# All heads' values as one operand (high halves, a one, 63 low halves), the 64th low half summed on DVE, and more gates beside both attentions

## The chip, the cores and the metric

The kernel runs on one core of a Trainium2 chip. The metric is device time in microseconds of one execution. TensorE (PE) multiplies, PEld is its weight load, VectorE (DVE), ScalarE (ACT) and GpSimd (POOL) do the rest, SyncE (SP) issues nearly all DMAs. Matmul results lie in PSUM, in eight banks of 128 partitions by 512 numbers; everything else is in SBUF.

## The reference

Two layers of an encoder over 512 tokens and 1024 channels, all in float32. What matters here, shortened:

```python
def block_attention(q, k, v):                     # softmax over 512 keys
    sc = einsum(q, k) * dk ** -0.5
    return einsum(softmax(sc), v)
for l in range(2):
    h = rms_norm(x, attn_norm_g[l])
    c_q, c_kv, k_rope, gq, gk, gv, pool_in, gate_logits = split_columns(h @ w_in[l], IN_SIZES)
    o_mla = mla_branch(...)      # 8 heads, keys of 64 + 32, values of 64, made from low-rank latents
    o_gqa = gqa_branch(...)      # 8 query heads of 64, 2 key/value heads
    o_pool = pool_branch(...)    # centred means over 2, 4, 8, 16 tokens
    gates = sigmoid(gate_logits)                  # three gates of 1024 channels
    merged = (gates[0] * (o_mla @ w_branch_mla[l]) + gates[1] * (o_gqa @ w_branch_gqa[l])
              + gates[2] * (o_pool @ w_branch_pool[l]))
    x = x + merged @ w_out[l]
    u = depthwise_conv(rms_norm(x, ffn_norm_g[l]) @ ffn_w_up[l])
    x = x + (silu(u_gate) * u_val) @ ffn_w_down[l]
```

## The kernel before

**Numbers in two halves.** Every operand of a matmul is split into a rounded high half (an `F32R` copy, mostly by ACT) and a low half (the number minus its high half, by DVE or POOL). A product is three matmuls, high x high, high x low and low x high: the helper `mm3`. A weight arrives by DMA in pieces of up to 512 columns, two to a load (`w_dma`, on SP's queue), three loads ahead; `w_split` makes its halves `wh` and `wl`, three pieces ahead.

**One order, planned when the program is built.** Instructions are issued by a Python program that keeps a clock of its own (`Clock`). It has an estimated cost for each instruction and a heap of later steps: `chain(...)` puts the steps that follow a matmul (an ACT copy, then a DVE subtraction, and so on) at the times when the estimates let them start; `need(key)` moves the clock to when something is ready, `ps(tag)` to when a PSUM bank is free. So the order on every engine is fixed beforehand, and on the chip each engine runs its own list and waits on semaphores. The banks are named by tag: `acc` two, `ST` two, `AV` two, `S` one, `mi` one.

**A layer.** The input projection comes first: latents, pool channels, GQA queries, and GQA keys and values (`tok_major` for results by token, `feat_major` for results by channel). The norm's sum of squares `sq` is reduced by eight small matmuls (`norm_finish`), in layer 0 during the first pool group. Then come the three branches, and then output projection, up-projection with convolution, and down-projection.

**The attentions.** `attention(kind, fill, ...)` runs 8 heads. A head transposes its queries (`t_q`, and `t_k` in MLA), finds row maxima from high halves alone (`s_max`: four matmuls into `S`, each followed by a DVE reduction `nm`), folds them in (`m_row`), and for each of four key blocks computes scores into an `ST` bank (`probs`), takes the exponential there on ACT (`ex`), copies the high half `ph` (`hi`) and subtracts for the low half `pl` (`lo`), after which the bank is free. `av_hi` multiplies the values' high halves by `ph`, and in a second matmul of 64 columns their low halves by `ph`; `av_lo` multiplies the high halves by `pl`. All 12 matmuls of a head go to one `AV` bank:

```python
                mm(s["av"], vh, ph[:, :T], k == 0, False)
                mm(s["av"][0:64], vl, ph[:, :T], False, False)
                mm(s["av"], vh, pl[:, :T], False, k == 3)
```

`vh` holds 64 columns of value high halves and 64 columns of ones, so rows 64 to 127 of the bank are the softmax's denominators. `o_out` copies both parts out, and after each second head transposes the sums, takes reciprocals, multiplies, and splits the pair into an operand `oh`, `ol` of the branch's projection.

**Fillers beside them.** A `Filler` is a list of independent matmul groups that is stepped between the attention's own: a unit is one step, three matmuls of 512 columns in a gate or a branch. `gates(br, ...)` makes, for one branch, 8 gates `gate(m)` (8 units; DVE multiplies by the norm, ACT takes a tanh) and 8 branch projections `branch(m)` (4 units; a DVE product, an addition to `XM`, in the last branch a split and a DMA back of the old `XM`), interleaved by `_order(br)` with MLA's making of queries, key parts and values (`EXTRA`). Branch 2 (pool) runs beside the GQA attention; branch 1 (GQA) and 16 units of branch 0 (MLA) beside the MLA attention; the other 80 units of branch 0 after it. Positions of an attention's steps relative to its heads are in `PLAN`: one position is a quarter of a head. A step whose inputs are not ready by the clock lets the filler go ahead, by up to `SLACK` units.

Of the kernel before, what the change touches and what calls it, by code (L numbers as in the profile page):

```python
# [11 lines left out]
F32R = mybir.dt.float32r  # L12
# [18 lines left out]
RAW = 3  # L31
EXTRA = (("q", 2, (2, 5)), ("n", 2, (6, 7)), ("v", 1, (0, 3)))
PRO = 0.47
# [6 lines left out]
PLAN = {"gqa": (0.006, 0.786, 0.986, 0.65, 3.252, 2.411, 4.57, 32.003),  # L40
        "mla": (-2.351, 0.028, 1.098, 0.64, 3.303, 1.678, 1.82, 33.91)}
W_BIAS = 2.54
C_BIAS = 0.2
# [13 lines left out]
def _order(br):  # L57


    r, lag = [], 2 if br == 0 else 1  # L60
# [127 lines left out]
class Engine:  # L188
# [35 lines left out]

    def tensor_scalar(self, out, *a):
        self._count(out, *((0.0043, 0.2) if self.kind == "Pool" else (0.00055, 0.07)))
        return self.eng.tensor_scalar(out, *a)
# [19 lines left out]
def trunk(ctx: ExitStack, tc: tile.TileContext, x, w, prm, gb, cst, out):  # L247
# [57 lines left out]
    def w_split():  # L305
        j = st["split"]
        sl, off, wd = pieces[j]
        r = raws[sl][:, off:off + wd]
        hi = hlp.tile([P, T], F32R, tag="wh", name=f"wh{j}")
        lo = hlp.tile([P, T], F32R, tag="wl", name=f"wl{j}")  # L310
        ck.fin = ck.now
        A.activation(hi[:, :wd], r, AF.Copy)
        e = V if j < KC + 3 else pick(W_BIAS, ck.fin + ck.SEM)
        ck.free[e.kind] = max(ck.free.get(e.kind, 0.0), ck.fin + ck.SEM)
        e.tensor_tensor(lo[:, :wd], r, f(hi[:, :wd]), ALU.subtract)
        done("w", j)
        halves[j] = (hi, lo)
        st["split"] += 1
# [45 lines left out]
    ones = cp.tile([P, P], F32R, tag="ones", name="ones")  # L364
    mhalf = cp.tile([P, 1], F32, tag="mhalf", name="mhalf")


# [142 lines left out]
    def layer(l, sq, xsrc):  # L510
# [172 lines left out]
        gqb = [ps(t) for t in qtags]  # L683
        VG, KAB = [], []
        for b in range(4):
            v = slot("vg", F32R)
            vh = v[:, 0:256].rearrange("p (h f) -> p h f", f=P)
            vl = v[:, 256:384].rearrange("p (h f) -> p h f", f=64)
            VG.append((vh, vl))
        for j in range(2):  # L690
            KAB.append((slot("ka", F32R), slot("kb", F32R)))

        def set_ones():
            for vh, _ in VG:
                V.memset(f(vh[:, :, 64:P]), 1.0)
            for _, kb in KAB:
                V.memset(f(kb[64:68, :T]), 1.0)
# [85 lines left out]
        def kv_evac(b):  # L783
            vh, vl = VG[b]
            src = kvb[b][:, P:2 * P].rearrange("p (h f) -> p h f", f=64)
            A.activation(vh[:, :, 0:64], src, AF.Copy, scale=rtok(b))
            A.activation(krt[:, b, :], kvb[b][:, 2 * P:288], AF.Copy, scale=rtok(b))

            def lo():
                V.scalar_tensor_tensor(vl, src, rtok(b), f(vh[:, :, 0:64]), ALU.mult, ALU.subtract)  # L790
                free(ktags[b])
                done("vg", l, b)
            chain(lo, after=ck.fin - ck.now + 0.1)
# [92 lines left out]
        mla_make = {}  # L886
        VM = {}
        ss = small("ssm", [P, 2, 2, 4, 4])
        krr = small("krr", [P, 4, 32], bufs=1)
# [121 lines left out]
        def v_out(g, p, acc):  # L1011
            lo2 = slot("vml", F32R)
            vs = []
            for i in range(2):
                v = slot("vmh", F32R)
                vh = v[:, :T].rearrange("p (h f) -> p h f", f=P)
                lv = lo2[:, 256 * i:256 * i + 256].rearrange("p (h f) -> p h f", f=64)
                G.memset(f(vh[:, :, 64:P]), 1.0)
                VM[2 * p + i, g] = (vh, lv)
                vs.append((vh[:, :, 0:64], lv, acc[:, 256 * i:256 * i + 256].rearrange("p (h f) -> p h f", f=64)))  # L1020

            def hi():
                for vh, _, src in vs:
                    copy(vh, src)
# [12 lines left out]
        def attention(kind, fill, okey, odst):  # L1037
# [27 lines left out]
            def t_pair(h):  # L1065
# [7 lines left out]
                for i in range(2):  # L1073
# [5 lines left out]
                    def hi(qa=qa, own=own):  # L1079
                        copy(qa[own, :T], tp[own])  # L1080

# [62 lines left out]
            def probs(h, k):  # L1144
# [23 lines left out]
                def lo():  # L1168
                    V.tensor_tensor(pl[:, :T], sc, f(ph[:, :T]), ALU.subtract)
                    free("ST")  # L1170
                    done(*key("pl", h, k))

                chain(ex, hi, lo)

            def vals(h, k):
                if gqa:
                    need(("vg", l, k))
                    vh, vl = VG[k]
                    return vh[:, h // 4, :], vl[:, h // 4, :]
                need(("vm", l, k, h // 4))  # L1180
                vh, vl = VM[k, h // 4]
                return vh[:, h % 4, :], vl[:, h % 4, :]

            def av_hi(h, k):
                s = hs[h]
                need(key("ph", h, k))
                if k == 0:
                    s["av"] = ps("AV")
                vh, vl = vals(h, k)
                ph = s["p", k][0]  # L1190
                mm(s["av"], vh, ph[:, :T], k == 0, False)
                mm(s["av"][0:64], vl, ph[:, :T], False, False)

            def av_lo(h, k):
                s = hs[h]
                need(key("pl", h, k))
                vh, vl = vals(h, k)
                pl = s.pop(("p", k))[1]
                mm(s["av"], vh, pl[:, :T], False, k == 3)
                if k == 3:  # L1200
                    o_out(h)

            def o_out(h):
# [6 lines left out]
                def copies():  # L1210
                    A.activation(sums[js, :T], s["av"][64:128], AF.Copy)
                    A.activation(raw[js, :T], s["av"][0:64], AF.Copy)
                    free("AV")

                steps = [copies]
                if h % 2 == 1:
# [4 lines left out]
                    steps += [lambda: V.transpose(turned[:, :T], sums[:, :T]),  # L1221
                              lambda: V.reciprocal(inv, turned[:, :T].rearrange("p (b f) -> p b f", f=32)[:, :, 0]),
                              lambda: V.transpose(sums[:, :T].rearrange("p (b f) -> p b f", f=32),
                                                  bc(inv.unsqueeze(2), [P, 16, 32]))]
# [7 lines left out]
            for h in range(8):  # L1232
# [11 lines left out]
            def waits(fn, h, k=None):  # L1244
# [11 lines left out]
                if fn is av_hi:  # L1256
                    return [key("ph", h, k)], "AV" if k == 0 else None
                return [key("pl", h, k)] * (fn is av_lo), None

# [17 lines left out]

        fa = Filler(gates(2, "op", opool, "first"), units(2))
        fa.upto(PRE_A)
# [9 lines left out]
        attention("gqa", fa, "og", ogqa)  # L1289
        fc = Filler(gates(0, "om", omla, "last"), units(0))  # L1290

        def beside():

            yield from gates(1, "og", ogqa, "add")
            for _ in range(2 * KC):
                fc.step()
                yield
# [6 lines left out]
        fc.finish()  # L1304

# [126 lines left out]
    A.activation(warm, warm, AF.Exp)  # L1432
    V.memset(f(ones), 1.0)
    idle = ps("mi")
    for _ in range(9):
# [163 lines left out]
```

## Time and profile before

| | |
|---|---|
| median of three runs | 1649.69 us (1648.71 to 1650.75) |
| the profiled execution | 1649.25 us, span of its instructions 1647.3 us |
| PE busy | 1640.4 us, 7435 matmuls |
| DVE, ACT, POOL busy | 890.5, 761.8, 921.9 us |
| HBM read | 139.90 MB, 87 GB/s over the span with what is written |

The span is the time from the first to the last instruction on the core. In a row of groups the columns are engine, operation, tiles written and read (out<-in), shapes, count, then busy time and mean duration in ns, then the engine's idle time just before and what ended it. In a row of the timeline they are start, duration (us), engine, line, operation, tiles, count; what stands in brackets is idle time of the engine before it and who released it. In a table of windows each engine has its busy us and its count of instructions in that stretch.

### The profile page before, as it was taken

The numbers are of one execution on the slowest core, as the hardware profiler recorded it, in microseconds if no ns is written. First come the engines' busy times: TensorE is split into PE (matmuls) and PEld (weight loads), VectorE is DVE, ScalarE is ACT, GpSimd is POOL, SyncE is SP. The second block draws the span as 40 slices with busy tenths as digits, with TensorE's granted clock in tenths as the row PEclk, the third lists the DMA queues.
The fourth block names the chain that finished last, engine by engine and source line by source line (L and its number), as shares of the span: only waits on it lengthen the run. The fifth ranks groups of instructions, "written<-read, shape, count | busy, mean of one in ns | idle before, by whom it ended". The sixth has DMA issues, their size and how long they took to land.

```text
span 1647.3 us, 20363 instructions
## 1 busy us (share of the span) xinstructions
PE 1640.4 (100%) x7435; PEld 1336.7 (81%) x7435; DVE 890.5 (54%) x1404; ACT 761.8 (46%) x1357; POOL 921.9 (56%) x805
## 2 busy tenths in 40 slices
PE   9999999999999999999999999999999999999999
PEld 8887887778888888888888888877788888888888
DVE  6777756643366666621046677566332666666000
ACT  6457745543444444432244577455434444444221
POOL 3762763344666666654568538534446656656542
PEclk9999999999999999999999999999999999999999
DMA  5221121123322323333332211211243232332331
GB/s 201 82 84 46 60 65 48 52 71 118 119 90 90 103 90 91 102 102 122 102 103 89 82 39 62 74 39 52 85 133 95 85 103 90 91 101 90 126 111 45
DMA packets 44739, 145.40 MB, mean 88 GB/s; under 512 B 5088, under 2 KB 6624, under 8 KB 44640
## 3 DMA queue, kind: packets, MB, share of 16 engines
q1 hardware_dynamic: 44352, 143.97, 27.6%
q8 instruction: 59, 0.97, 0.2%
q14 instruction: 40, 0.33, 0.1%
q10 hardware_dynamic: 288, 0.14, 0.0%
HBM read 139.90 MB, written 4.19 MB: 87 GB/s over the span
## 4 chain that ended last, share of the span: by engine, by line
PE 98%; DVE 1%; ACT 1%; DMA 0%; SPq 0%; issue 0%
PE ps_acc L344 44%; PE ps_AV L344 24%; PE ps_ST L344 23%; PE ps_S L344 4%; PE ps_mi L344 2%; PE ps_mi L348 1%; DVE sq L215 0%; DMA XM<-x 0%; ACT wh L208 0%; ACT sqt L208 0%; DVE wl L215 0%; PE ps_acc L348 0%; SPq L301 0%; ACT HH L208 0%; SPq L1439 0%
## 5 line engine op out<-in xcount | busy, mean ns | idle before, releaser
L215 POOL TENSOR_TENSOR wl<-raw,wh 128x512 fp32r<-128x512 f32 (+2 forms) x508 | 662.9, 1315 | 589.0 <-ACT wh L208 457.7
L208 ACT ACTIVATE wh<-raw 128x512 fp32r<-128x512 f32 (+3 forms) x522 | 308.8, 607 | 125.6 <-PE ps_ST L344 41.1
L219 DVE SCALAR_TENSOR_TENSOR a<-u,prm,a 128x512 f32<-128x512 f32 x176 | 238.9, 1358 | 79.4 <-ACT a L208 73.2
L344 PE MATMUL ps_acc<-HH,wh 128*128 128x512 f32 x592 | 234.7, 396 | 1.4 <-DVE XM L219 1.4
L344 PE MATMUL ps_acc<-HL,wh 128*128 128x512 f32 x592 | 234.6, 396 | 0.0
L344 PE MATMUL ps_acc<-HH,wl 128*128 128x512 f32 x592 | 234.2, 396 | 0.0
L344 PEld LDWEIGHTS ps_acc<-HH,wh 128*128 128x128 f32 x592 | 111.5, 188 | 28.5 <-ACT mqs L208 1.7
L344 PEld LDWEIGHTS ps_acc<-HH,wl 128*128 128x128 f32 x592 | 111.3, 188 | 26.3
L344 PEld LDWEIGHTS ps_acc<-HL,wh 128*128 128x128 f32 x592 | 111.5, 188 | 25.5
L208 ACT ACTIVATE ps_ST<-ps_ST 128x512 f32<-128x512 f32 x128 | 74.6, 583 | 113.5 <-PE ps_ST L344 113.0
L344 PE MATMUL ps_AV<-HL,wh 128*128 128x512 f32 x288 | 114.2, 396 | 0.0
L344 PE MATMUL ps_AV<-HH,wl 128*128 128x512 f32 x288 | 114.2, 396 | 0.0
L344 PE MATMUL ps_AV<-HH,wh 128*128 128x512 f32 x288 | 113.6, 394 | 0.0
L223 DVE TENSOR_REDUCE nm<-ps_S 128x1 fp32r<-128x512 f32 x128 | 87.8, 686 | 42.4 <-PE ps_S L344 41.1
L215 DVE TENSOR_TENSOR pl<-ps_ST,ph 128x512 fp32r<-128x512 f32 x128 | 87.7, 685 | 38.4 <-ACT ph L208 37.4
L215 POOL TENSOR_TENSOR al<-a,ah 128x512 fp32r<-128x512 f32 x44 | 58.2, 1322 | 84.9 <-ACT ah L208 58.6
L344 PE MATMUL ps_ST<-HL,wh 128*128 128x512 f32 x240 | 95.3, 397 | 0.0
L344 PE MATMUL ps_ST<-HH,wl 128*128 128x512 f32 x240 | 95.0, 396 | 0.0
L344 PE MATMUL ps_ST<-HH,wh 128*128 128x512 f32 x240 | 94.6, 394 | 0.0
L208 ACT ACTIVATE a<-u,prm 128x512 f32<-128x512 f32 x88 | 71.8, 815 | 33.4 <-DVE u L215 33.4
L208 ACT ACTIVATE ah<-a 128x512 fp32r<-128x512 f32 x44 | 27.8, 631 | 116.0 <-DVE u L243 110.6
L208 ACT ACTIVATE a<-a 128x512 f32<-128x512 f32 x44 | 27.8, 632 | 113.0 <-DVE u L243 113.0
(361 smaller groups left out, 3543.8 us busy)
## 6 DMA issues: line engine op xcount, KB each, us to landing
raw<-w SPq DMA_DIRECT2D x228, 512.0 KB, 3.5
raw<-w SPq DMA_DIRECT2D x13, 384.0 KB, 3.1
XM<-x SPq DMA_DIRECT2D x16, 256.0 KB, 4.1
raw<-w SPq DMA_DIRECT2D x6, 448.0 KB, 3.4
xsp<-XM SPq DMA_DIRECT2D x8, 256.0 KB, 2.0
XM<-xsp SPq DMA_DIRECT2D x8, 256.0 KB, 3.4
out<-XM SPq DMA_DIRECT2D x7, 256.0 KB, 2.1
raw<-w SPq DMA_DIRECT2D x4, 432.0 KB, 3.1
```

Source lines behind the costliest of these rows:

```text
L208: return self.eng.activation(out, in_, func, **k)
L215: return self.eng.tensor_tensor(out, *a)
L219: return self.eng.scalar_tensor_tensor(out, *a)
L223: return self.eng.tensor_reduce(out, in_, *a, **k)
L344: PE.matmul(o, lhsT=lhsT, rhs=rhs, start=start, stop=stop)
L348: PE.transpose(o, src, ident)
```

## The change

Values: `vh` becomes one operand of 128 columns: 64 high halves, a single column of ones (64), and the low halves of value channels 1 to 63 (65 to 127). The low half of channel 0 goes to a small tile (`vg0`, `vm0`). `av_hi` and `av_lo` are one matmul each with this operand. Row 64 of the bank is then the denominator and rows 65 to 127 hold what is to be added to rows 1 to 63. The contribution of the 64th low half is summed over the key blocks by DVE from the scores in PSUM (`rest`, before the `ST` bank is freed) into a tile `t`, and one more matmul with `unit`, a matrix whose first column is ones, adds it to row 0 (`av_rest`). `o_out` sets the denominators' row in the copied lower part to zero, after the reciprocals, and adds it to the raw output (on GpSimd, for the last head on DVE); two small ACT copies spread the reciprocals.

Fillers: 24 units of branch 1 move beside the GQA attention, and 48 instead of 16 units of branch 0 stand beside the MLA attention (`SOONER`), with gates running further ahead of their projections (`LAG`), and the MLA values made with other gates (`EXTRA`).

Smaller edits: the first weight piece's high half is copied by DVE; for that piece (`use == 1` in `tok_major`: the first of eight channel blocks of layer 0's latents) the twelve matmuls run operand by operand, not bank by bank; layer 0's `norm_finish` comes two units later; the GQA queries' high half is always copied by ACT; `set_ones` and MLA's memsets write one column for 64.

```diff
-EXTRA = (("q", 2, (2, 5)), ("n", 2, (6, 7)), ("v", 1, (0, 3)))
+EXTRA = (("q", 2, (2, 5)), ("n", 2, (6, 7)), ("v", 1, (2, 5)))
+SOONER = {1: 3 * KC, 0: 6 * KC}
+LAG = {2: 1, 1: 4, 0: 6}
...
-        A.activation(hi[:, :wd], r, AF.Copy)
+        if j == 0:
+            V.tensor_copy(hi[:, :wd], r)
+        else:
+            A.activation(hi[:, :wd], r, AF.Copy)
...
+                if st["use"] == 1:
+                    for n, (x_, w_) in enumerate(((HH, wh), (HL, wh), (HH, wl))):
+                        for b in range(4):
+                            mm(banks[b][:, :wd], x_[:, kc, b * P:b * P + P], w_[:, :wd], n == 0, False)
+                    continue
...
-                if l == 0 and g == 0 and n == 3:
+                if l == 0 and g == 0 and n == 5:
...
-                for vh, lv, src in vs:
-                    V.tensor_tensor(lv, src, f(vh), ALU.subtract)
+                for vh, v0, src in vs:
+                    V.tensor_tensor(vh[:, :, 65:P], src[:, :, 1:64], f(vh[:, :, 1:64]), ALU.subtract)
+                for vh, v0, src in vs:
+                    V.tensor_tensor(v0, src[:, :, 0], f(vh[:, :, 0]), ALU.subtract)
...
-                        copy(qa[own, :T], tp[own])
+                        A.activation(qa[own, :T], tp[own], AF.Copy)
...
                 def lo():
                     V.tensor_tensor(pl[:, :T], sc, f(ph[:, :T]), ALU.subtract)
+                    done(*key("pl", h, k))
+                def rest():
+                    if k == 0:
+                        s["t"] = slot("vt", F32R)
+                        V.tensor_scalar(s["t"][:, :T], sc, vals(h, k)[1], None, ALU.mult, psum=True)
+                    else:
+                        t = s["t"][:, :T]
+                        V.scalar_tensor_tensor(t, sc, vals(h, k)[1], f(t), ALU.mult, ALU.add)
                     free("ST")
-                    done(*key("pl", h, k))
+                    if k == 3:
+                        done(*key("t", h))
-                chain(ex, hi, lo)
+                chain(ex, hi, lo, ([("vg", l, k) if gqa else ("vm", l, k, h // 4)], rest))
...
-                mm(s["av"], vh, ph[:, :T], k == 0, False)
-                mm(s["av"][0:64], vl, ph[:, :T], False, False)
+                mm(s["av"], vals(h, k)[0], s["p", k][0][:, :T], k == 0, False)
...
+            def av_rest(h):
+                s = hs[h]
+                need(key("t", h))
+                mm(s["av"], unit, s["t"][:, :T], False, True)
+                o_out(h)
...
+                def add():
+                    for j in (0, 64):
+                        G.memset(sums[j:j + 1, :T], 0.0)
+                    (V if h == 7 else G).tensor_tensor(raw[:, :T], raw[:, :T], sums[:, :T], ALU.add)
...
+                    steps += [add, lambda: (A.activation(inv[32:64], inv[0:32], AF.Copy),
+                                            A.activation(inv[96:128], inv[64:96], AF.Copy))]
...
+                plan.append((p0 + 7 + al + REST, av_rest, (h,)))
...
+        rest = {br: Filler(gates(br, *a), units(br)) for br, a in ((1, ("og", ogqa, "add")), (0, ("om", omla, "last")))}
+        def beside(now, br):
+            yield from now
+            for _ in range(SOONER[br]):
+                rest[br].step()
+                yield
-        fa = Filler(gates(2, "op", opool, "first"), units(2))
+        fa = Filler(beside(gates(2, "op", opool, "first"), 1), units(2) + SOONER[1])
...
-        fb = Filler(beside(), units(1) + 2 * KC)
+        fb = Filler(beside(left(rest[1]), 0), units(1) - SOONER[1] + SOONER[0])
```

More of the change, by code (lines that the diff above doesn't have):

```diff
@@ L41 @@
         "mla": (-2.351, 0.028, 1.098, 0.64, 3.303, 1.678, 1.82, 33.91)}
+REST = 0.4
 W_BIAS = 2.54
@@ L57, in _order @@
 def _order(br):
[L60 removed]
+    r, lag = [], LAG[br]
     for m in range(KC + lag):
@@ L684, in layer @@
         VG, KAB = [], []
+        vg0 = small("vg0", [P, 4, 2])
         for b in range(4):
             v = slot("vg", F32R)
-            vh = v[:, 0:256].rearrange("p (h f) -> p h f", f=P)
-            vl = v[:, 256:384].rearrange("p (h f) -> p h f", f=64)
-            VG.append((vh, vl))
+            VG.append((v[:, 0:256].rearrange("p (h f) -> p h f", f=P), vg0[:, b]))
         for j in range(2):
@@ L887, in layer @@
         VM = {}
+        vm0 = small("vm0", [P, 4, 8])
         ss = small("ssm", [P, 2, 2, 4, 4])
@@ L1011, in v_out @@
         def v_out(g, p, acc):
-            lo2 = slot("vml", F32R)
             vs = []
             for i in range(2):
-                v = slot("vmh", F32R)
+                b = 2 * p + i
+                v = slot("vm", F32R)
                 vh = v[:, :T].rearrange("p (h f) -> p h f", f=P)
[L1017 to L1020, printed above, removed]
+                G.memset(f(vh[:, :, 64:65]), 1.0)
+                v0 = vm0[:, b, 4 * g:4 * g + 4]
+                VM[b, g] = (vh, v0)
+                vs.append((vh, v0, acc[:, 256 * i:256 * i + 256].rearrange("p (h f) -> p h f", f=64)))
             def hi():
                 for vh, _, src in vs:
-                    copy(vh, src)
+                    copy(vh[:, :, 0:64], src)
             def lo():
-                for vh, lv, src in vs:
-                    V.tensor_tensor(lv, src, f(vh), ALU.subtract)
+                for vh, v0, src in vs:
+                    V.tensor_tensor(vh[:, :, 65:P], src[:, :, 1:64], f(vh[:, :, 1:64]), ALU.subtract)
+                for vh, v0, src in vs:
+                    V.tensor_tensor(v0, src[:, :, 0], f(vh[:, :, 0]), ALU.subtract)
                 free("acc")
@@ L1169, in lo @@
                     V.tensor_tensor(pl[:, :T], sc, f(ph[:, :T]), ALU.subtract)
+                    done(*key("pl", h, k))
[5 more added lines that the diff above has]
+                        t = s["t"][:, :T]
+                        V.scalar_tensor_tensor(t, sc, vals(h, k)[1], f(t),
+                                               ALU.mult, ALU.add)
                     free("ST")
-                    done(*key("pl", h, k))
-                chain(ex, hi, lo)
+                    if k == 3:
+                        done(*key("t", h))
+                chain(ex, hi, lo, ([("vg", l, k) if gqa else ("vm", l, k, h // 4)], rest))
             def vals(h, k):
@@ L1177, in vals @@
                     need(("vg", l, k))
[L1178 to L1179 removed]
+                    vh, v0 = VG[k]
+                    return vh[:, h // 4, :], v0[:, h // 4:h // 4 + 1]
                 need(("vm", l, k, h // 4))
[L1181 to L1182 removed]
+                vh, v0 = VM[k, h // 4]
+                return vh[:, h % 4, :], v0[:, h % 4:h % 4 + 1]
             def av_hi(h, k):
@@ L1221, in o_out @@
                     steps += [lambda: V.transpose(turned[:, :T], sums[:, :T]),
-                              lambda: V.reciprocal(inv, turned[:, :T].rearrange("p (b f) -> p b f", f=32)[:, :, 0]),
-                              lambda: V.transpose(sums[:, :T].rearrange("p (b f) -> p b f", f=32),
+                              lambda: V.reciprocal(inv, turned[:, :T].rearrange("p (b f) -> p b f", f=32)[:, :, 0])]
+                    steps += [add, lambda: (A.activation(inv[32:64], inv[0:32], AF.Copy),
+                                            A.activation(inv[96:128], inv[64:96], AF.Copy))]
+                    steps += [lambda: V.transpose(sums[:, :T].rearrange("p (b f) -> p b f", f=32),
                                                   bc(inv.unsqueeze(2), [P, 16, 32]))]
@@ L1257, in waits @@
                     return [key("ph", h, k)], "AV" if k == 0 else None
-                return [key("pl", h, k)] * (fn is av_lo), None
+                return [key("t", h)] if fn is av_rest else [key("pl", h, k)], None
             def waiting(fn, *args):
@@ L1276, in units, with left @@
             return sum(UNITS[k] for k, _ in _order(br))
-        fa = Filler(gates(2, "op", opool, "first"), units(2))
+        rest = {br: Filler(gates(br, *a), units(br)) for br, a in ((1, ("og", ogqa, "add")), (0, ("om", omla, "last")))}
[4 more added lines that the diff above has]
+                yield
+        def left(fill):
+            while fill.step():
+                yield
+            fill.finish()
+        fa = Filler(beside(gates(2, "op", opool, "first"), 1), units(2) + SOONER[1])
         fa.upto(PRE_A)
@@ L1289, in layer @@
         attention("gqa", fa, "og", ogqa)
[L1290 to L1297, printed above, removed]
-        fb = Filler(beside(), units(1) + 2 * KC)
+        fb = Filler(beside(left(rest[1]), 0), units(1) - SOONER[1] + SOONER[0])
         fb.upto(PRE_B)
@@ L1433, in trunk @@
     V.memset(f(ones), 1.0)
+    G.memset(f(unit), 0.0)
+    G.memset(f(unit[:, 0:1]), 1.0)
     idle = ps("mi")
```

23 lines of the change are left out of this document (10 added, 13 removed).

## The prediction

> **What bounds the kernel now.** I read the page first (busy time of each engine, then the chain that ended last), then the chain in order of time, then the busy time by stage, and last the timeline around each place where TensorE stops.
>
> ```profile
> span 1647.3 us, 20363 instructions
> PE 1640.4 (100%) x7435; PEld 1336.7 (81%) x7435; DVE 890.5 (54%) x1404; ACT 761.8 (46%) x1357; POOL 921.9 (56%) x805
> PE 98%; DVE 1%; ACT 1%; DMA 0%; SPq 0%; issue 0%
> ```
>
> The chain is TensorE for 98% of the span. A busy PE need not be a full one, since matmuls overlap; what tells is the distance between starts, and that is constant:
>
> ```profile
> 353.89 63.27 PE ps_acc L344 x273
> 479.89 5.60 PE ps_ST L344 x24
> 703.89 15.27 PE ps_acc L344 x66
> ```
>
> 63.27/273 = 0.2318 us, 5.60/24 = 0.2333, 15.27/66 = 0.2314. So a 512-column matmul costs 0.232 us, and the kernel is a row of them with next to nothing between. A matmul taken away is worth that much, if the other engines keep up. Here are the busy times (DVE third, ACT fourth, POOL fifth) of the GQA attention of layer 0, its MLA attention, the gates left after it, and the GQA attention of layer 1:
>
> ```profile
> core 0: us, PE busy (x) PEld busy (x) DVE busy (x) ACT busy (x) POOL busy (x), PEclk, DMA share, GB/s
> 105.00:214.00 109.00, 107.56 (x496) 86.54 (x495) 78.08 (x124) 75.78 (x138) 59.48 (x77) 1.00 0.18 54
> 238.00:354.00 116.00, 116.00 (x538) 92.31 (x537) 72.59 (x118) 65.05 (x118) 47.54 (x44) 1.00 0.15 47
> 354.00:417.00 63.00, 63.00 (x274) 51.06 (x272) 24.98 (x36) 23.33 (x41) 28.99 (x23) 1.00 0.38 120
> 922.00:1031.00 109.00, 109.00 (x506) 88.14 (x505) 80.41 (x128) 76.94 (x140) 61.29 (x79) 1.00 0.17 54
> ```
>
> DVE is busy 72 to 74% of the GQA attention, 63% of the MLA attention and 40% of the gates behind it. That is the room for the new DVE work.
>
> **The matmuls removed.** For each head and key block the values take three matmuls now: high halves, the 64-column low halves, and the probabilities' low half. After the change it is two, and one more per head for the summed column: 12 become 9. With 8 + 8 heads and 2 layers, 32 x 3 = 96 matmuls go. Does the narrow one cost a full slot?
>
> ```profile
> 353.03 0.40 PE L344 MATMUL ps_AV<-ph,vmh 128*128 128x512 f32 x1
> 353.26 0.39 PE L344 MATMUL ps_AV<-ph,vml 128*64 128x512 f32 x1
> 353.50 0.39 PE L344 MATMUL ps_AV<-pl,vmh 128*128 128x512 f32 x1
> ```
>
> It starts 0.23 after the wide one and the next 0.24 after it: a full slot, whatever its width. 96 x 0.232 = **-22.3 us** (22.2 to 22.4 by the three pitches). The Trainium skill, "TensorE: Matmul & The Clock Gate", section "Wait — 56ns, not 53.3ns?", gives 215.7 ns from start to start for 512 columns; by it the term would be 20.7 us. This trace never shows the main stream below 0.231, so the measured pitch stands.
>
> **What DVE takes on.** A new pass for each head and key block reads the probabilities from PSUM, scales them by one column and adds them up in SBUF. Nearest rows, all with one PSUM operand and 512 columns:
>
> ```profile
> L215 DVE TENSOR_TENSOR pl<-ps_ST,ph 128x512 fp32r<-128x512 f32 x128 | 87.7, 685 | 38.4 <-ACT ph L208 37.4
> L219 DVE SCALAR_TENSOR_TENSOR gt<-gt,ps_acc 128x512 f32<-128x512 f32 x32 | 21.8, 681 | 28.7 <-PE ps_acc L344 28.5
> ```
>
> So 0.685 each, 128 of them: 87.7 us, 21.9 in each of the four attentions. It lies beside TensorE as long as DVE has room. The moved gates make the stages longer or shorter. In the GQA attention 24 matmuls (5.6 us) go, and 24 units from branch 1 come: two gates and six units of a third (22 x 3 x 0.232 = 15.3) and two half-width value units (12 x 0.116, an estimate of half the pitch, 1.4). 109 becomes 120 us. DVE gets 21.9 for the sums, about 2 for three gates' logits (0.69 each) and about 2 for the value splits: 78.1 + 26 = 104, or 86%. In the MLA attention 5.6 and those 16.7 go and 32 units of branch 0 come (22.3): still 116 us; DVE 72.6 + 22.6 = 95, or 82%. The gates behind it shrink from 63 to 41 us. What the moved gates bring to the other queues: 6 weight pieces to GQA (ACT and POOL one split each, SP half a load each), which the 0.18 DMA share takes easily. POOL gets beside them the sum of raw and column (1.30 a pair) and two one-row memsets:
>
> ```profile
> L215 POOL TENSOR_TENSOR oraw<-oraw,osum 128x512 f32<-128x512 f32 x12 | 15.6, 1297 | 7.1 <-DVE osum L239 6.9
> L243 POOL MEMSET kh<- 4x512 f32 x16 | 8.3, 520 | 0.9
> ```
>
> About 2.3 a pair and 9 an attention; with the 6 low halves (1.3 each) POOL goes from 59 to some 77 of 120. ACT gets the query copies that DVE shared before, and two tiny ones a pair: some 84 of 120. Neither becomes the bound. I cost all this at nothing; the cover is DVE's free 14 to 18%.
>
> **What stalls at that load.** One row of before shows how a late DVE reaches TensorE:
>
> ```profile
> 150.00 0.34 PE L344 MATMUL ps_acc<-wh,ctl 128*128 128x384 f32 x1
> ...
> 151.78 0.47 PE L344 MATMUL ps_acc<-HH,wh 128*128 128x512 f32 x1 [1.44 <-DVE XM L219]
> ```
> ```profile
> 150.23 0.68 DVE L215 TENSOR_TENSOR qa<-ps_mi,qa 64x512 fp32r<-64x512 f32 x1
> ...
> 150.94 0.69 DVE L219 SCALAR_TENSOR_TENSOR XM<-gt,ps_acc 128x512 f32<-128x512 f32 x1
> ```
>
> The product that frees a `ps_acc` bank queued behind another DVE instruction, and TensorE, in order, lost 1.78 - 0.17 = 1.6 us. The new pass is one more thing for `logits`, `product` and `nm` to queue behind. Bounds: nothing (the layer 1 attention above, 74% DVE, has PE busy 109.00 of 109), and one such stall a head, 32 x 1.6 = 51 us. The stages will be at 82 to 86%, not saturated, and the order is planned around DVE's expected delays, so I stay near the lower end: one more in each GQA attention, **+3.2 us**.
>
> **The ST bank.** It is now freed after the new pass:
>
> ```profile
> 182.30 0.39 PE L344 MATMUL ps_ST<-qa,ka 128*128 128x512 f32 x1
> ...
> 182.97 0.58 ACT L208 ACTIVATE ps_ST<-ps_ST 128x512 f32<-128x512 f32 x1 [0.24 <-PE ps_ST L344]
> ...
> 183.58 0.60 ACT L208 ACTIVATE ph<-ps_ST 128x512 fp32r<-128x512 f32 x1
> ...
> 184.50 0.68 DVE L215 TENSOR_TENSOR pl<-ps_ST,ph 128x512 fp32r<-128x512 f32 x1
> ```
>
> 2.9 us from first matmul to free, 3.7 with the pass (and a hop of 0.1). There are two banks and 32 uses in 110 to 120 us, one in 3.4 or more: a bank has 6.8 us. Covered; zero.
>
> **The end of an attention.** The last head's output must be ready for branch 0. Now:
>
> ```profile
> 353.93 0.59 ACT L208 ACTIVATE osum<-ps_AV 64x512 f32<-64x512 f32 x1 [2.83 <-PE ps_AV L344]
> ```
> ```profile
> 358.83 0.69 DVE L215 TENSOR_TENSOR ol<-oraw,oh 128x512 fp32r<-128x512 f32 x1 [0.70 <-ACT oh L208]
> ```
> ```profile
> 361.43 0.39 PE L344 MATMUL ps_acc<-oh,wh 128*128 128x512 f32 x1
> ```
>
> It takes 5.6 us; the last pair is the fourth operand, 9 matmuls (2.1) after 361.43, so 4.0 us are spare. The change adds two memsets (1.0), an add on DVE (0.7), two small copies and hops (0.6): 2.3. The last matmul comes 0.4 of a block later (1.4). 0.3 is left: zero, at worst 1 us a layer.
>
> **The start.** The sum of squares is now waited for two units later:
>
> ```profile
> 25.17 0.40 PE L344 MATMUL ps_AV<-HH,wl 128*128 128x512 f32 x1
> 26.18 1.05 PE L344 MATMUL ps_S<-ones,sq 128*128 128x2 f32 x8 [0.61 <-DVE sq L215]
> ```
>
> 1.01 between starts against 0.23: **-0.8 us**; six matmuls (1.4) now cover it. The first weight piece is split on DVE, and its matmuls are reordered around its late low half. What is late next is the second piece:
>
> ```profile
> 5.79 0.45 PE L344 MATMUL ps_acc<-wl,HH 128*128 128x384 f32 x1 [0.16 <-DVE wl L215]
> ```
> ```profile
> 7.50 0.55 DVE L215 TENSOR_TENSOR wl<-raw,wh 128x384 fp32r<-128x384 f32 x1
> ```
> ```profile
> 8.10 0.44 PE L344 MATMUL ps_acc<-wl,HH 128*128 128x384 f32 x1
> ```
>
> It ends at 8.05 and TensorE takes it at 8.10, as early as it can. What is won before 8 is waited for there: zero (at most 0.5).
>
> **The sum.** The profiled execution took 1649.25 (span 1647.3 and 1.95 around it), 0.4 below the median of 1649.69. 1649.25 - 22.3 - 0.8 + 3.2 = 1629.35, say **1629.3 us**.
>
> **The rivals.**
> (1) DVE's queue costs TensorE much more. For: 86% is a mean, and the plan puts several things on DVE at once; the `ps_acc` stall is there at 72%. Against: it is one in four attentions. At one 1.6-us stall in every second head's worth of GQA work and one in four of MLA (8 + 4 = 12 of them, 19 us) nearly all would be lost; half of that, 10 us, gives 1636.
> (2) Slower: the ST bank. If the new pass waits so long in DVE's queue that a bank comes round after more than 6.8 us, each of 128 blocks waits for it. The point is 3.1 us of queueing on top of 3.7; 22.3 + 0.8 is used up by 0.18 us a block, and 0.3 us a block gives 1649.25 - 23.1 + 38.4 = 1664.6. Against: 3.1 us are over four DVE instructions ahead of it.
> (3) The clock falls in the stalls. The nine first matmuls take 4.21 us, twice the later pitch:
> ```profile
> 1.10 4.21 PE L1436 MATMUL ps_mi<-ones 128*128 128x512 f32 x9 [1.10 <-DVE ones L243]
> ```
> If a stall brought that back, for as long, each would cost 2.1 us more; six of them on top of (1) give 1649. Against: granted clock 1.00 in the window with the 1.6-us stall. The Trainium skill, "TensorE: Matmul & The Clock Gate", section "Part 1: The HAM clock gate", puts the drop to half rate after an idle window of about 3.4 us; the trace has no such stall behind the start.
> (4) Better than the sum: no stall is new and the one at 150 goes too: 1649.25 - 22.3 - 0.8 - 1.6 = 1624.6.
> (5) The change doesn't do what it says, the narrow matmul having been nearly free: 1649. The 0.23 spacing excludes it almost.
>
> **Chances and range.** Forecast (1625.5 to 1633) 0.66; (1) 0.20; (2) 0.04; (3) 0.02; (4) 0.06; (5) 0.02. 0.2%, or 3.3 us, is about what a measurement of this kernel tells from no change; (1) and (4) are faster. Faster 0.93, same 0.03, slower 0.04. The range 1625 to 1639 holds the forecast, a third of (4) and most of (1), some 0.82.
>
> **What would show it.** In the profile after: 96 fewer PE matmuls (7339); a group of 128 DVE instructions into the new sum at about 0.69; the two attentions of a layer some 120 and 116 us long with DVE at 80 to 87%; the gap at 25 gone and the one at 8 still there; 40 us of gates behind MLA. PE waits in the attentions should sum to under 5 us, on `ps_acc` released by DVE. The prediction is wrong if the new instruction costs much more than 0.69, if TensorE waits there for ST or S banks, or if the pitch between matmuls rises with the changed mix.

## The result, and the profile after

The changed kernel takes 1626.96 us in the median (1626.90 to 1627.04), against 1649.51 for the kernel before (1648.71 to 1650.75): a ratio of 0.9864, 95% interval 0.9852 to 0.9877. That is 22.5 us less; the forecast was 1629.3, from 1625 to 1639.

The page after, the same rows as before:

```profile
span 1625.0 us, 20404 instructions
PE 1619.4 (100%) x7339; PEld 1323.9 (81%) x7339; DVE 982.6 (60%) x1562; ACT 768.5 (47%) x1389; POOL 949.0 (58%) x849
PE 99%; DVE 0%; ACT 0%; DMA 0%; issue 0%
```

7339 matmuls are 96 fewer. The span fell by 22.3 us, 0.232 for each. TensorE is still the whole chain. The stages, with the columns as before: GQA attention, MLA attention and the gates behind it of layer 0, GQA attention of layer 1.

```profile
core 0: us, PE busy (x) PEld busy (x) DVE busy (x) ACT busy (x) POOL busy (x), PEclk, DMA share, GB/s
105.00:224.00 119.00, 118.96 (x547) 96.95 (x547) 100.19 (x164) 81.77 (x156) 77.08 (x99) 1.00 0.19 61
248.00:363.80 115.80, 115.80 (x529) 93.38 (x529) 93.27 (x148) 65.40 (x119) 55.86 (x51) 1.00 0.17 53
363.80:404.00 40.20, 40.20 (x175) 32.35 (x174) 25.57 (x33) 17.24 (x31) 18.87 (x16) 1.00 0.40 131
922.00:1034.00 112.00, 110.97 (x509) 90.31 (x508) 95.58 (x158) 78.52 (x148) 71.31 (x94) 1.00 0.20 62
```

DVE is busy 84% of the GQA attention (100.2 of 119) and 81% of the MLA one, and TensorE hardly noticed. What TensorE waited for, all of it that the view of waits lists (columns: us in total, times, longest):

```profile
PE ps_mi L1481 <- DVE ones L247: 1.1, 1, 1.1
PE ps_acc L351 <- DVE XM L223: 1.0, 2, 0.6
PE ps_acc L351 <- DVE wh L235: 0.3, 1, 0.3
```

The first and third are the opening; 1.0 us in two waits is left to the attentions. Both lie in layer 1 and look like the stall of before: a `ps_acc` bank whose DVE product comes late. Here is the longer one in TensorE's rows and in DVE's, where the product `XM` stands behind the new pass:

```profile
983.50 0.28 PE L351 MATMUL ps_acc<-wh,ctl 128*128 128x256 f32 x1
...
984.37 0.50 PE L351 MATMUL ps_acc<-HH,wh 128*128 128x512 f32 x1 [0.59 <-DVE XM L223]
```
```profile
982.98 0.74 DVE L231 TENSOR_SCALAR vt<-ps_ST,vg 128x512 fp32r<-128x512 f32 x1
983.64 0.68 DVE L223 SCALAR_TENSOR_TENSOR XM<-gt,ps_acc 128x512 f32<-128x512 f32 x1
```

The new pass itself in the GQA attentions (`vt` is its sum; the rows of MLA, with `vm`, have 735 and 739 ns):

```profile
L223 DVE SCALAR_TENSOR_TENSOR vt<-ps_ST,vg,vt 128x512 fp32r<-128x512 f32 x48 | 35.6, 742 | 0.2
L231 DVE TENSOR_SCALAR vt<-ps_ST,vg 128x512 fp32r<-128x512 f32 x16 | 11.9, 744 | 0.1
```

Each takes 0.74 us, not 0.685, the first instruction of a head no less than the three that add to it.

### The profile page after: what moved, and what is told of

The parts are those of the page before. It is cut to its first block, busy times and chain, and to the rows that moved or that the text cites. A ratio compares the mean times of both kernels' runs of the same rounds, so it can differ in the third digit from the quotient of the medians.

```text
span 1625.0 us, 20404 instructions
## 1 busy us (share of the span) xinstructions
PE 1619.4 (100%) x7339; PEld 1323.9 (81%) x7339; DVE 982.6 (60%) x1562; ACT 768.5 (47%) x1389; POOL 949.0 (58%) x849
## 4 chain that ended last, share of the span: by engine, by line
PE 99%; DVE 0%; ACT 0%; DMA 0%; issue 0%
PE ps_acc L351 45%; PE ps_ST L351 24%; PE ps_AV L351 23%; PE ps_S L351 4%; PE ps_mi L351 2%; PE ps_mi L355 1%; DMA prm<-prm 0%; PE ps_acc L355 0%; DVE XM L223 0%; DVE nm L227 0%; DVE pl L219 0%; ACT qa L212 0%; PE ps_S L355 0%; PE ps_ST L355 0%; DVE HL L223 0%
## 5 line engine op out<-in xcount | busy, mean ns | idle before, releaser
L219 POOL TENSOR_TENSOR wl<-raw,wh 128x512 fp32r<-128x512 f32 (+3 forms) x506 | 663.2, 1320 | 540.0 <-ACT wh L212 434.5
L212 ACT ACTIVATE wh<-raw 128x512 fp32r<-128x512 f32 (+1 forms) x521 | 309.4, 608 | 126.3 <-PE ps_ST L351 40.3
L351 PEld LDWEIGHTS ps_acc<-HL,wh 128*128 128x128 f32 x592 | 111.4, 188 | 25.2
```

The lines of the kernel that those rows point to most:

```text
L212: return self.eng.activation(out, in_, func, **k)
L219: return self.eng.tensor_tensor(out, *a)
L351: PE.matmul(o, lhsT=lhsT, rhs=rhs, start=start, stop=stop)
```

## The experiments

My theory was that the time is the count of matmul slots, and that DVE's pass is hidden as long as the moved gates give it room. The rivals: the gates bring a gain of their own; the pass is hidden whatever stands beside it; the longer holding of the `ST` bank costs; the narrow matmul was cheap.

### The gate moves alone

```diff
 # the kernel before, with
+EXTRA = (("q", 2, (2, 5)), ("n", 2, (6, 7)), ("v", 1, (2, 5)))
+SOONER = {1: 3 * KC, 0: 6 * KC}
+LAG = {2: 1, 1: 4, 0: 6}
...
+        fa = Filler(beside(gates(2, "op", opool, "first"), 1), units(2) + SOONER[1])
+        fb = Filler(beside(left(rest[1]), 0), units(1) - SOONER[1] + SOONER[0])
```

> The kernel before with the filler moves alone (24 units of branch 1 beside the GQA attention, 48 of branch 0 beside MLA, gates running further ahead, MLA values made with other gates); the values' three matmuls a block stay. Slot theory (the time is the count of 512-column matmuls by 0.232 us, and the moves only give DVE room): no matmul goes, so 1648 to 1650, at best 1.6 us less if the stall at 150 us goes. Rival (part of the 22.5 us comes from the better mix of fillers): 1635 to 1645.

Measured: 1648.12 us, ratio 0.9991 (0.9982 to 1.0001). By themselves the moves are worth nothing that stands clear of the noise; the fillers' mix is no source of the gain.

### The new values alone

```diff
 # the changed kernel, with
-SOONER = {1: 3 * KC, 0: 6 * KC}
-LAG = {2: 1, 1: 4, 0: 6}
...
-        fa = Filler(beside(gates(2, "op", opool, "first"), 1), units(2) + SOONER[1])
+        fa = Filler(gates(2, "op", opool, "first"), units(2))
...
+        fb = Filler(beside(), units(1) + 2 * KC)
```

> The changed kernel with the fillers as before (16 units of branch 0 beside MLA, none of branch 1 beside GQA). The GQA attention would have 109 - 5.6 = 103 us, and DVE 78.1 + 32 x 0.742 = 102 in it (98%); MLA 110 us and DVE 96 (87%). Slot theory in its plain form (DVE's pass is hidden anyway): 1626 to 1628, as the changed kernel. Cover theory (the pass is hidden only because the moved gates give DVE time): TensorE waits for DVE in the GQA attentions, 4 to 12 us in all, so 1631 to 1639, on ps_acc, ps_S or ps_ST released by DVE.

Measured: 1655.22 us, ratio 1.0037 (1.0023 to 1.0051). With 96 matmuls fewer it is slower than the kernel before. The cover theory is right in kind and was far too small in size: 28 us more than the changed kernel, not 4 to 12. Where it goes is seen in the windows of this kernel's second GQA attention (the last 16 us with fillers, then its end):

```profile
core 0: us, PE busy (x) PEld busy (x) DVE busy (x) ACT busy (x) POOL busy (x), PEclk, DMA share, GB/s
1000.00:1016.00 16.00, 16.00 (x75) 12.89 (x75) 15.03 (x25) 12.33 (x23) 13.95 (x23) 1.00 0.21 67
1016.00:1042.00 26.00, 20.91 (x71) 13.15 (x69) 21.97 (x39) 17.81 (x32) 18.58 (x21) 0.87 0.00 0
```

In the first stretch DVE is at 94% and TensorE loses nothing. In the second the fillers are used up, and TensorE issues 71 matmuls in 26 us, some 60% of the pace before, with DVE at 85%. The changed kernel still has fillers in the last 16 us of the same attention, and there TensorE is full beside a DVE at 82% (same columns):

```profile
1016.00:1032.00 16.00, 16.00 (x76) 12.88 (x75) 13.12 (x26) 12.49 (x25) 12.64 (x16) 1.00 0.19 58
```

The timeline of the stretch without fillers, TensorE alone:

```profile
1023.38 0.40 PE L349 MATMUL ps_S<-ka,qa 128*128 128x512 f32 x1
1025.28 0.50 PE L349 MATMUL ps_ST<-qa,ka 128*128 128x512 f32 x1 [1.50 <-DVE vt L229]
...
1029.32 0.63 PE L349 MATMUL ps_AV<-pl,vg 128*128 128x512 f32 x1
1029.74 0.63 PE L349 MATMUL ps_AV<-vt,unit 128*128 128x512 f32 x1
```

First come waits for DVE: for the `S` bank behind a reduction `nm`, and above all for an `ST` bank that the pass holds, 1.9 us from start to start at the longest. After a few of them some 13 matmuls go on at 0.43 us, without a wait, at half the pace; the window's granted clock is 0.87. Summing for each stage what the matmuls' starts lie apart beyond the usual distance of their shape (my sum over the trace), this kernel loses 7 and 10 us more than the changed one in its GQA attentions, 4 and 4 in the MLA ones and 2.5 and 1 behind these.

### Only one of the two moves

```diff
-SOONER = {1: 3 * KC, 0: 6 * KC}
+SOONER = {1: 0, 0: 6 * KC}        # MLA's move only
+SOONER = {1: 3 * KC, 0: 2 * KC}   # GQA's move only
```

> The changed kernel without the 24 units of branch 1 beside the GQA attention (they run beside MLA), but with 48 units of branch 0 beside MLA. The kernel with all moves undone was 28 us slower than the changed one, its stalls lying 7 and 10 us in the GQA attentions, 8 in the MLA ones and 4 behind. Theory (each attention needs its own fillers, and loses where they run out): the GQA part comes back, MLA's not: 1640 to 1647. Rival (the loss is one of DVE's total load, spread over all): half way or less, 1627 to 1636, or all of it, 1652 to 1656.

Measured: 1644.10 us, ratio 0.9970 (0.9959 to 0.9982), 17 us more than the changed kernel. The same sum over the trace finds 16 of these 17 us in the two GQA attentions and nothing in MLA, so each attention pays for its own fillers. This run also parts the waits from the clock. The end of its second GQA attention, without fillers, in the same columns:

```profile
1010.00:1029.00 19.00, 13.21 (x49) 7.62 (x48) 17.18 (x28) 12.87 (x24) 15.10 (x22) 1.00 0.00 0
```

49 matmuls in 19 us are some 55% of the pace with fillers, DVE is at 90%, and the granted clock is 1.00. The two GQA attentions thus lose nearly as much here as in the kernel with the new values alone (16 against 17 us), with no fall of the clock: the waits for DVE make the loss.

> The changed kernel with the 24 units of branch 1 beside the GQA attention, but 16 units of branch 0 beside MLA as before the change, not 48. Theory (each attention loses where its own fillers run out): the GQA attentions as in the changed kernel; the MLA ones, with 32 units (22 us) less, worse than in the kernel with both moves undone (their 24 units of branch 1 are gone too): 8 to 25 us more than the changed kernel, 1635 to 1652. Rival (MLA's 80% load leaves room enough): 1627 to 1630.

Measured: 1660.05 us, ratio 1.0065 (1.0048 to 1.0083), 33 us more than the changed kernel, 8 above the top of the expectation. Its GQA attentions are as in the changed kernel; the MLA attentions lose 15 to 16 us each. The windows at the end of the first one:

```profile
315.00:330.00 15.00, 13.94 (x65) 10.87 (x64) 12.74 (x21) 9.71 (x19) 8.52 (x10) 1.00 0.22 70
330.00:345.00 15.00, 10.59 (x37) 6.75 (x35) 13.17 (x22) 7.54 (x15) 2.49 (x4) 0.89 0.00 0
345.00:365.00 20.00, 17.95 (x55) 12.49 (x56) 11.18 (x18) 9.33 (x17) 7.71 (x7) 0.74 0.10 27
```

Fillers last until about 330. Then DVE is at 88% and TensorE issues 57% of its matmuls, and in the last stretch the granted clock is 0.74. Of what this attention loses, the lower clock can have cost at most 7 us (0.11 of 15 us and 0.26 of 20). The waits for DVE's reductions lead here, not those on `ST`:

```profile
PE ps_mi L351 <- DVE nm L227: 6.1, 4, 1.8
PE ps_S L351 <- DVE nm L227: 5.7, 8, 1.2
```

Leaving one move out thus costs 17 us (GQA's) or 33 us (MLA's), and leaving out both costs 28, not the sum: without GQA's move its 24 units stand beside MLA and cover there. To a kernel without the pass the moves are worth nothing.

### The narrow matmul by itself

```diff
-                mm(s["av"][0:64], vl, ph[:, :T], False, False)
```

> The kernel before without the 64-column matmul of the values' low halves (their part of the result is left out); everything else as before. It prices the narrow matmul by itself: 128 go. Slot theory: 128 x 0.232 = 29.7 us, so 1619 to 1621. Rival (a matmul with half the columns costs little, and the 22.5 us came from elsewhere): 1640 to 1650.

Measured: 1624.05 us, ratio 0.9846 (0.9831 to 0.9862), 25.2 us less than the 1649.2 of the kernel before in these runs. That is short of 29.7 by 4.5 us, and the trace has them: its GQA attentions, shorter with the same DVE work, lose 1.5 and 3.1 us more than before. So the narrow matmul did cost a whole slot; nearly free, as the rival had it, is out.

### The pass twice, and no pass

```diff
                 def rest():
                     ...
+                        V.scalar_tensor_tensor(t2, sc, vals(h, k)[1], f(t2), ALU.mult, ALU.add)
                     free("ST")
```

> The changed kernel with DVE's new pass made a second time into a tile that nothing reads, before the ST bank is freed: 128 x 0.74 = 95 us more on DVE, 23.8 in each attention, no matmul more. DVE would be asked for 124 us in a GQA attention of 119 and 117 in an MLA attention of 116. Slot theory with cover: DVE becomes the bound in both, at least 2 x 5 us, and with the waits between 15 and 40 us: 1642 to 1667. Rival (DVE is far from mattering, its queue is never waited for): under 3 us, 1627 to 1630. Rival (ST bank: 0.74 us more of holding in each block is what costs): the waits of TensorE would be on ps_ST, not on ps_acc or ps_S.

Measured: 1680.08 us, ratio 1.0186 (1.0168 to 1.0204), 53 us more than the changed kernel, beyond the expected 15 to 40. Its waits:

```profile
PE ps_ST L351 <- DVE vt L223: 8.0, 10, 1.7
PE ps_ST L351 <- DVE vt L231: 4.6, 4, 2.0
PE ps_mi L351 <- DVE nm L227: 4.4, 4, 2.0
PE ps_S L351 <- DVE nm L227: 3.9, 6, 1.1
```

The `ST` bank leads, as the rival said, and the DVE reductions follow. With both added, this does not tell a long holding from a late DVE. The run with GQA's move only says more: there the reductions lead with 11.8 us, and waits on `ST` behind the pass sum to 1.7, so a late DVE is enough without the `ST` bank.

```diff
-                chain(ex, hi, lo, ([("vg", l, k) if gqa else ("vm", l, k, h // 4)], rest))
+                chain(ex, hi, lo)
...
-                plan.append((p0 + 7 + al + REST, av_rest, (h,)))
```

> The changed kernel without DVE's pass and without the matmul that adds it (the 64th low half is left out of the result); moved gates stay. 32 matmuls fewer: -7.4 us. Theory (DVE's pass at 80 to 84% load costs TensorE only some 2 us of stalls): 1627.0 - 7.4 - 0 to 3 = 1616.5 to 1620. Rival (the pass costs TensorE 10 us or more that are hidden in the result): under 1612.

Measured: 1618.39 us, ratio 0.9812 (0.9798 to 0.9827), 8.6 us less than the changed kernel. 32 matmuls are 7.4, so 95 us of DVE work in the attentions cost TensorE 1.2 us.

### The pass from SBUF

```diff
-                        V.scalar_tensor_tensor(t, sc, vals(h, k)[1], f(t), ALU.mult, ALU.add)
+                        V.scalar_tensor_tensor(t, f(ph[:, :T]), vals(h, k)[1], f(t), ALU.mult, ALU.add)
 # the first block's tensor_scalar likewise; free("ST") already behind lo
```

> The changed kernel with DVE's pass reading the probabilities' high half ph from SBUF in place of the scores in PSUM (the 64th low half is then multiplied by the high half alone, as the narrow matmul did before); the ST bank is freed before the pass. ST-bank theory (the longer holding costs TensorE): faster, 1624 to 1626. Load theory: the bank has time enough, so what counts is the length of the pass. With 0.74 us as now: 1626 to 1628. With two SBUF inputs beside a busy POOL it may take up to the 1.36 us of the row a<-u,prm,a: DVE then has 120 us in a GQA attention of 119, and 1635 to 1655.

Measured: 1635.58 us, ratio 0.9919 (0.9904 to 0.9934), 8.6 us more than the changed kernel. Freeing the bank earlier did not pay, since the pass became longer; what the bank alone is worth stays open (columns: shortest, median and longest in ns):

```profile
L223 DVE SCALAR_TENSOR_TENSOR vt<-ph,vg,vt x48: 734/850/1829, 120.5 to 1037.2; 128x512 fp32r<-128x512 f32 x48
L223 DVE SCALAR_TENSOR_TENSOR vt<-ph,vm,vt x48: 658/1088/1868, 258.2 to 1177.7; 128x512 fp32r<-128x512 f32 x48
L231 DVE TENSOR_SCALAR vt<-ph,vg x16: 466/488/942, 118.6 to 1027.6; 128x512 fp32r<-128x512 f32 x16
```

With one SBUF input it is faster (0.49), with two it is anything from 0.66 to 1.87. It goes with POOL: by the start and end times in this trace, the 17 adding passes that no POOL instruction overlaps took 0.66 to 0.75, and the 79 others 0.73 to 1.87, 1.16 in the median. The Trainium skill, "SBUF — State Buffer", section "SBUF: two separate sides", says that a DVE instruction with two SBUF inputs and a GpSimd one that reads SBUF lock each other out for a whole instruction. The trace fits that: POOL's subtractions here last 1.3 us, and a pass of 0.7 that waits for most of one comes to the upper end. In the changed kernel, with scores from PSUM, the pass stays between 0.66 and 0.75.

### The start

```diff
 # the changed kernel, with all three edits undone (first), or the last two (second)
-                if l == 0 and g == 0 and n == 5:
+                if l == 0 and g == 0 and n == 3:
-            V.tensor_copy(hi[:, :wd], r)
+            A.activation(hi[:, :wd], r, AF.Copy)
-                if st["use"] == 1:
+                if st["use"] == -1:
```

> The changed kernel with the three edits at the start undone (sum of squares reduced two units earlier, first piece's high half on ACT, first twelve matmuls bank by bank). Theory: the reduction's gap of 0.8 us comes back and the other two are worth nothing, since the second piece's low half at 8.05 us decides: 1627.5 to 1628.1. Rival (the first matmuls also count): 1628.3 to 1629.5. Rival (nothing counts): 1627.0.

> The changed kernel with the first piece's high half on ACT and the first twelve matmuls bank by bank as before, but the sum of squares still reduced two units later. The three edits at the start together were worth nothing; the trace shows the reduction's gap of 0.6 us gone and the first matmul 0.5 us later. If both readings hold: 0.3 to 0.6 us less than the changed kernel, 1626.3 to 1626.7. If the reduction's gap is hidden by something later: 1627.0.

Measured: 1626.95 and 1626.97 us, ratios 0.9865 (0.9849 to 0.9882) and 0.9864 (0.9849 to 0.9878). In both the theory failed and the other reading held, that nothing is gained (1627.0): no edit at the start can be told from the changed kernel's 1626.96. In that kernel's trace the gap before the reduction is gone, and the first matmul comes later (5.61, before the change 5.11):

```profile
5.61 0.59 PE L351 MATMUL ps_acc<-wh,HH 128*128 128x384 f32 x2 [0.30 <-DVE wh L235]
...
8.09 0.44 PE L351 MATMUL ps_acc<-wl,HH 128*128 128x384 f32 x1
```
```profile
26.55 0.40 PE L351 MATMUL ps_AV<-HH,wl 128*128 128x512 f32 x1
26.79 0.95 PE L351 MATMUL ps_S<-ones,sq 128*128 128x2 f32 x8
```

With all three undone the gap was 0.6 us, and in other kernels with the old start 0.4 and 0.5; by my sum the opening then loses 0.4 us more than in the changed kernel, and the rest of that execution 0.5 less. Differences of that size are within what executions spread, and what each edit is worth stays open.

### A planner with the measured costs

```diff
-        ck.to(ck.now + max(0.107, rhs.shape[-1] / 2370.0))
+        ck.to(ck.now + max(0.107, rhs.shape[-1] / 2210.0))
 # and DVE on PSUM 0.00105 -> 0.0012 us an element (0.0013 with a column), ACT 0.00084 -> 0.00098, POOL 0.002145 -> 0.0023
```

> The changed kernel with the planner's estimated costs set to what the trace shows (512-column matmul 0.232 us for 0.216, DVE on PSUM 0.685 for 0.61, with a column 0.74, ACT 0.59 for 0.52, POOL 1.30 for 1.23). The order on each engine changes, no instruction does. Theory (what is left in the attentions is some 1.2 us of waits behind DVE that a better order can at most take away): 1625.5 to 1627.5. Rival (the order was fitted to the old figures): 1628 to 1634.

Measured: 1628.49 us, ratio 0.9872 (0.9858 to 0.9887): 1.5 us more. Its GQA attentions lose 1.8 us less, but the last pair of heads comes too late for branch 0:

```profile
371.20 0.40 PE L351 MATMUL ps_acc<-oh,wl 128*128 128x512 f32 x1
372.22 0.50 PE L351 MATMUL ps_acc<-oh,wh 128*128 128x512 f32 x1 [0.63 <-ACT oh L212]
```
```profile
365.32 0.25 DVE L239 RECIPROCAL oinv<-otr 128x16 f32<-128x16 f32 x1
368.76 0.69 DVE L219 TENSOR_TENSOR oraw<-oraw,osum 128x512 f32<-128x512 f32 x1 [3.19 <-POOL osum L247]
```

The second DVE row waits 3.2 us for POOL's two memsets, which run at 367.6, behind a weight's low half. So the last kernel has, besides,

```diff
-                        G.memset(sums[j:j + 1, :T], 0.0)
+                        (V if h == 7 else G).memset(sums[j:j + 1, :T], 0.0)
```

> The kernel with the planner's costs matched to the trace, and for the last pair of heads the two one-row memsets on DVE in place of POOL. That kernel (matched costs alone) had 1.8 us less of stalls in the GQA attentions than the changed one and lost 2 x 1.9 us behind the MLA attentions, where the last pair of heads comes too late: DVE waits 3.2 us there for POOL's memsets, which queue behind a weight split. Theory (that queue is the cause): the 3.8 us go, 1624.5 to 1626, the fastest of all. Rival (the end of MLA is late whatever does the memsets): 1627.5 to 1629.

Measured: 1626.14 us (1625.87 to 1626.86), ratio 0.9864 (0.9847 to 0.9880). 2.4 of the 3.8 us that the expectation named came back, and the time is just above the expected band: the end of MLA is no longer late (the memsets' queue was the cause), and 0.5 us of waits for `mgl`, the low half that the output projection needs, stay. Against the changed kernel it is 0.8 us less, 0.05%, which the intervals don't tell apart: a tie.

## Why the prediction was right

**The matmuls removed: right.** 96 went, the pitch stayed (15.28/66 = 0.2315 after), and the narrow one's full slot, read from two starts of 0.23, held in the run that left it out.

```profile
691.00 15.28 PE ps_acc L351 x66
```

The span fell by 22.3 us, the term's own size; that it agrees to the tenth is luck, since by my sum over the trace what was lost (1.3 us in the GQA attentions, 0.5 in other places) and what was won (0.9 at the start, 0.9 between the attentions) cancel.

**DVE's load: right, from a wrong duration.** The pass takes 0.74, not 0.685: 94.6 us in all. The nearest row was not the product `gt` but the instructions with a per-partition column and PSUM in one; before, `qb<-ps_mi,gcol,qa` took 0.726 on 96 partitions. The shares still came out at 84 and 81% against 86 and 82, since other parts were put too high: two errors that happened to cancel.

**The stalls: the term that was mis-sized.** 3.2 us were put in. The run without the pass prices them at 1.2, and by my sum over the trace the two GQA attentions lose 1.3 us more than before (the old 1.6-us stall in layer 0 shrank to 0.2, new ones came in layer 1). The place was right: `ps_acc`, behind DVE, in the GQA attention. A smaller gain was not in the sum at all: between the attentions TensorE loses 0.9 us less, since MLA's value splits no longer stand there. Of before:

```profile
PE ps_acc L344 <- DVE vml L215: 0.4, 2, 0.2
```

These two make the forecast's 2.3 us too many (1.9 + 0.9, less 0.5 elsewhere).

**The start: right in the trace, not to be seen in the time.** The opening loses 0.9 us less in the profiled execution (0.8 forecast), but undoing its edits cost nothing that can be measured. The second piece did decide at 8.09, as the prediction had it.

**The cover: named wrongly.** The prediction hid DVE's pass under "DVE's free 14 to 18%". The runs showed another thing: at 94% with fillers TensorE loses nothing, at 85 to 90% without them it loses 40 to 45% of its pace. What hides the pass is independent matmuls until the end of each attention, so that TensorE has something to do while DVE catches up. The moved gates, which I costed as a change of DVE's share, are what decides the sign: 28 us, more than the change's whole gain. The prediction came out although it did not say this, because the gates were part of the change; in that it was lucky.

**The ST bank: zero was right, the margin small.** Counted as in the prediction, from a block's first matmul to the end of the pass, the bank is held 4.5 us in the mean, not 3.7, and 6.8 at most. The longest are in MLA, where 32 blocks in 116 us on two banks leave each 7.2. TensorE still never waits for it. Rival (2) is real in other kernels: without the moved gates, and with the pass twice, TensorE's waits are longest in sum on `ps_ST`, released by `vt`, and both kernels are slower than before.

**The end of an attention: right.** The chain now lasts 8.1 us (expected 7.9) and is over 0.7 us before the first matmul on this pair:

```profile
363.87 0.59 ACT L212 ACTIVATE osum<-ps_AV 64x512 f32<-64x512 f32 x1 [3.72 <-PE ps_AV L351]
```
```profile
371.33 0.69 DVE L219 TENSOR_TENSOR ol<-oraw,oh 128x512 fp32r<-128x512 f32 x1 [0.76 <-ACT oh L212]
```
```profile
372.77 0.39 PE L351 MATMUL ps_acc<-oh,wh 128*128 128x512 f32 x1
```

**The clock: right for this change.** It did not fall in the changed kernel (1.00 in every window above). It did in the profiled executions of three kernels in which TensorE ran out of fillers (both moves left out, MLA's left out, the pass twice), so the rival exists. The kernel with MLA's move only lost 16 us without it: the waits come first, and the fall is at most a part of the loss.

## What to carry to other kernels

On a core whose TensorE never waits, a matmul taken away is worth its slot (here 0.23 us, for 64 columns of values as for 128), but only if the work that replaces it has matmuls of other parts beside it until its very end. A mean load of the helping engine says little: look at the last stretch of the stage, where the fillers run out, and move independent work there first. Price a new instruction by the row with the same operands, the scalar column included.

## What the runs showed of the hardware that I had not expected

TensorE's pace can halve without a long gap: in the kernel with the new values alone the longest distance between starts was 1.9 us, and some 13 matmuls then ran at 0.43 us each with nothing to wait for. The Trainium skill, "TensorE: Matmul & The Clock Gate", section "Part 1: The HAM clock gate", puts the drop after an idle window of about 3.4 us; here no single gap was so long. What sets it off stays open: the kernel with MLA's move only had much the same waits in the same place, also 1.9 us from start to start at the longest, and its granted clock stayed at 1.00. A DVE pass that adds from two SBUF inputs beside a busy POOL took from 0.66 to 1.87 us, the same from PSUM and SBUF 0.66 to 0.75. A DVE memset of one row of 512 took 0.49 us, about as long as POOL's 0.52.
